# Expert 0's turn in the mixture of experts: 64 slots with fp32 products on unsplit weights, where it had 128 slots with split weights

## The chip, the cores and the metric

The kernel runs on one core of a Trainium2 chip. The time is that of the device, in microseconds, from the first to the last instruction of one execution with what lies around it; times are medians of several executions. One execution was recorded by the hardware profiler, and all rows below come from it.

## The reference

A decoder trunk of two layers over 256 tokens of width 1024, all in fp32. Each layer has a token-mixing part and then a channel mixer; the channel mixer of the second layer is a mixture of eight experts, of which each token uses its best two:

```python
logits = h @ router
top_v, top_i = lax.top_k(logits, 2)
wts = softmax(top_v)
combine = sum(one_hot(top_i, 8) * wts[..., None], axis=-2)
for e in range(8):
    y = y + combine[:, e:e+1] * ((silu(h @ w1[e]) * (h @ w3[e])) @ w2[e])
```

Here `w1[e]` and `w3[e]` are 1024 by 3584 and `w2[e]` is 3584 by 1024, so one expert has 44 MB of weights and all eight have 352 MB. Each weight is read once. With the reference's own inputs (its default seed) the reference gives the experts 0 to 7 these numbers of tokens: 60, 58, 49, 84, 77, 59, 69, 56.

## The kernel before

The mixture of experts is the function `moe`. It runs after everything else and takes the last half of the time. It works through eight **turns**, one expert each. Turn 0 is always expert 0, because its weights are fetched before the routing is known. The other seven experts are sorted by their number of tokens on the chip, and the table `RANK` gives each later turn a place in that order.

A turn gathers its expert's tokens into **slots** by a one-hot matrix `Pm`. There are two kinds of turn, told apart by `SMALL`:

- A *large* turn has 128 slots. Its weights are split by ScalarE and VectorE into a high and a low part (`hi`, `lo`, lines 1187 and 1188), and TensorE makes three fp32r products for each piece (lines 1408 to 1410 and 1426 to 1428).
- A *small* turn has 64 slots (`CAP`). It multiplies the fp32 weights as they landed (`raw`) with fp32 activations (`xs`, `as`), two halves of 64 columns of the array for each piece (lines 1404 and 1423). Nothing is split.

Before the change turns 0, 2, 4, 6 are large and 1, 3, 5, 7 small. Two neighbouring turns share one gather and one matrix `Pm` (`GROUPS`); the gather for the next pair is spread over the last step of a large turn. If an expert has more tokens than its turn has slots, all is computed again by a slow general path (`spill`); with the numbers above it isn't entered.

A turn has seven steps j, and a step three matrices (`w1`, `w3`, and `w2` of the step before), each in two **blocks** of 1 MB: 42 blocks a turn, 336 in all, numbered here from 0 in the order of their fetch. SyncE (SP) issues the transfers one after the other, in an order that the program text fixes. A block goes into one of 15 places `raw0` to `raw14`, or, once each at the start, into `acts`, `late` and `y`, which are used for other things later: 18 blocks are fetched ahead (`FIRST`), then never more than 15 are held (`MOE_BUFS`). A place comes free in a large turn when VectorE has written the block's last `lo`, in a small turn when TensorE has multiplied its last piece; `done` then fetches the next block:

```python
def fetch(most=MOE_BUFS):
    while todo and len(live) < most:
        n = slots.pop(0)
        ...
        nc.sync.dma_start(w, A["moe"][expert[e], j, b][:, h * 2048:(h + 1) * 2048])
```

For turns 1 to 7 `expert[e]` is a register. SP loads all seven from `idxi`, which VectorE computes (line 1304); this load (line 1312) stands in SP's queue between the fetches, and those behind it wait for it. Small work (the sort, the gather, the activation of a step) is laid between the pieces by a count of **ticks**, a tick for each half block multiplied. TensorE, VectorE, ScalarE and SP run in the order of the program text in this stage.

Of the kernel before, what the change touches and what calls it, by code (L numbers as in the profile page):

```python
# [9 lines left out]
F32 = mybir.dt.float32  # L10
# [4 lines left out]
ALU = mybir.AluOpType  # L15
# [3 lines left out]
P = 128  # L19
T = 256  # L20
D = 1024
KC = 8
# [5 lines left out]
NE = 8  # L28
# [29 lines left out]
NPRE = len(PRE)  # L58


RANK = [7, 0, 4, 1, 5, 2, 6, 3]
SMALL = [False, True] * 4
CAP = 64
NSMALL = sum(SMALL)
GROUPS = [(None, 0), (1, 2), (3, 4), (5, 6), (7, None)]


def constants():
    c = np.zeros((P, NCST), np.float32)

    def put(n, a):
        c[:a.shape[0], COFF[n][0]:COFF[n][0] + a.shape[1]] = a
# [10 lines left out]
    put("keyc", np.broadcast_to(np.array([1e6, 1, 2, 3, 4, 5, 6, 7])[None, :], (P, 8)))  # L83
    put("seq", np.broadcast_to(np.array(RANK)[None, :], (P, 8)))
    gmask = ((s <= t) & (i[:, None] // 64 == i[None, :] // 64)).astype(np.int32)
# [1048 lines left out]
def moe(k, l, out):  # L1134
    tc, nc, A = k.tc, k.nc, k.A
    ctx = ExitStack()
    dp = ctx.enter_context(tc.tile_pool(name="moe", bufs=1, reuse_waits="tile"))
# [31 lines left out]
    def done(block):  # L1169

        block[2] = True
        while live and live[0][2]:
            live.pop(0)
            fetch()

    def prepare(eng=nc.vector):
# [5 lines left out]
        last = q == 2048 // SUB - 1  # L1182
        if SMALL[at[0]]:
            ready.append((w[:, s], None, at + (q,), block if last else None))
# [6 lines left out]
        if last:  # L1191
            part.clear()
            blocks.pop(0)
            if not SMALL[at[0]]:
                done(block)
# [3 lines left out]
    def parts(n, kind=F32):  # L1199

        if n not in held:
            held[n] = sp.tile([P, 4, 512], kind, name=n)
        return held[n]
# [20 lines left out]
    n8, key, rank, more, idx = [S8[:, i] for i in range(5)]  # L1224
# [66 lines left out]
    def sort():  # L1291

        by = lambda a: a[:, None, :].to_broadcast([P, NE, NE])
        of = lambda a: a[:, :, None].to_broadcast([P, NE, NE])
        p, w = perm[:, 0], perm[:, 1]

        def ranks():
            nc.vector.scalar_tensor_tensor(key, n8, 8.0, k.k("keyc"), ALU.mult, ALU.add)
            nc.vector.tensor_tensor(w, of(key), by(key), ALU.is_gt)
            nc.vector.tensor_reduce(rank, w, AX.X, ALU.add)  # L1300
            nc.vector.tensor_tensor(p, by(rank), of(k.k("seq")), ALU.is_equal)
            nc.vector.tensor_tensor(w, p, by(iota[:, :NE]), ALU.mult)
            nc.vector.tensor_reduce(idx, w, AX.X, ALU.add)
            nc.vector.tensor_copy(idxi, idx)

        def turned(src, dst):
            for tt in range(2):
                nc.vector.tensor_tensor(w, p, by(src[:, tt]), ALU.mult)
                nc.vector.tensor_reduce(dst[:, tt], w, AX.X, ALU.add)

        def loads():
            _, v = nc.values_load_multi_w_load_instructions(idxi[0:1, 1:NE], engines=[mybir.EngineType.SP], min_val=0,
                                                            max_val=NE - 1)
            expert.extend(v)

        def excess():
            nc.vector.tensor_scalar(more, rank, NSMALL - 0.5, float(P - CAP), ALU.is_le, ALU.mult)
            nc.vector.tensor_tensor(n8, n8, more, ALU.add)
            nc.vector.tensor_reduce(cnt, n8, AX.X, ALU.max)
            nc.vector.tensor_copy(cnti, cnt)  # L1320

        return [ranks, loads, lambda: turned(posm, posm_s), lambda: turned(comb, comb_s), excess]
# [3 lines left out]
    def after(ticks, f):  # L1326

        tasks.append((clock[0] + ticks, f))
        tasks.sort(key=lambda t: t[0])

    def tick():
        clock[0] += 1
        while tasks and tasks[0][0] <= clock[0]:
            tasks.pop(0)[1]()

    def slots_of(g):

        Pm = dp.tile([P, 2, 2, P], F32R, name="Pm", bufs=2)
        for i, (t, io) in enumerate(zip(GROUPS[g], (iod, iota))):
            if t is not None:  # L1340
# [6 lines left out]
    def back(g, Pm, gs, PT):  # L1347
        pg = k.pg()
        here = [i for i in range(2) if GROUPS[g][i] is not None]
        for i in here:  # L1350
            for tt in range(2):
                t = GROUPS[g][i]
                c = comb_s[:, tt, t:t + 1] if t else comb[:, tt, 0:1]
# [9 lines left out]

    def places(g):

        xs = dp.tile([P, KC, CAP], F32, name="xs") if GROUPS[g][0] is not None else None
        xl = [dp.tile([P, KC, P], F32R, name=n) for n in ("xh", "xl")] if GROUPS[g][1] is not None else None
        return xs, xl

# [16 lines left out]
    def pieces(e, j, b):  # L1386
        for h in range(2):
            for q in range(2048 // SUB):
                while blocks and len(ready) <= LOOK:
                    prepare()  # L1390
                hi, lo, at, block = ready.pop(0)
                assert at == (e, j, b, h, q)
                yield (h * 2048 + q * SUB) // 512, hi, lo
                if block:
                    done(block)
                tick()

    def up(e, j, b, p, x):
        for o, hi, lo in pieces(e, j, b):
            for z in range(SUB // 512):  # L1400
                kc = o + z
                if SMALL[e]:
                    for n in range(2):
# [8 lines left out]
    def down(e, j, py, act):  # L1412
        if j == 0:
            py += [k.pc() for _ in range(1 if SMALL[e] else 2)]
        for o, hi, lo in pieces(e, j, 2):
            for n in range(2):
                for z in range(SUB // 1024):
                    c = o // 2 + z
                    s = slice(z * 1024 + n * 512, z * 1024 + n * 512 + 512)
                    first, last = j == 0 and c == 0, j == NJ - 1 and c == 3  # L1420
                    if SMALL[e]:
                        a = (c % 2) * P + (c // 2) * CAP
# [164 lines left out]
    def busy(n):  # L1587

        for _ in range(n):
            nc.tensor.matmul(idle[:, :T], ident, k.cst[:, :T], start=True, stop=True)  # L1590
# [4 lines left out]
    with tc.manual_schedule(engines=ORDERED | LOADS):  # L1595
        y = choose()
        idle = k.pj()
        busy(IDLE[0])
        pp = place()
        busy(IDLE[1])  # L1600
        for c in range(3):
            rows_of(c, y)
        rows_of(0, y, True)
        nc.vector.tensor_tensor(posm, posm, pp[:, 0:2 * NE].rearrange("p (a b) -> p a b", a=2), ALU.add)
        new = slots_of(0)
        nc.vector.tensor_copy(n8, pp[:, 2 * NE:3 * NE])
        rows_of(1, y, True)
        rows_of(2, y, True)
        to = places(0)
        for kc in range(KC):  # L1610
            gather(0, new[1], kc, to, k.pj if kc % 4 > 1 else k.pg)
        weigh()
        after(BACK, lambda: back(*new))
        for n, f in enumerate(sort()):
            after(SORT + n, f)
        group = new, to
        for e in range(NE):
            i = 0 if SMALL[e] else 1
            if e and i == 0:
                group = nxt  # L1620
            (_, _, gs, PT), (xs, x2) = group
            for j in range(NJ):
                ph = [k.pj()]
                up(e, j, 0, ph[0], x2 if i else xs)
                act, steps = hidden(e, ph)
                delay = DELAY
                if (e, j) == (NE - 1, NJ - 1):
                    delay, last = LAST, gains()
                after(delay[0], steps[0])
                ph.append(k.pj())  # L1630
                up(e, j, 1, ph[1], x2 if i else xs)
                for d, f in zip(delay[1:], steps[1:]):
                    after(d, f)
                if i == 1 and e < NE - 1:
                    g = e // 2 + 1
                    if j == NJ - 2:
                        new = slots_of(g)
                        after(BACK, lambda: back(*new))
                    if j == NJ - 1:
                        nxt = new, places(g)  # L1640
                        for kc in range(KC):
                            after(kc * 2048 // SUB // 4, lambda kc=kc, g=g, n=nxt: gather(g, n[0][1], kc, n[1]))
                if pend:
                    down(*pend[:4])
                    if pend[4]:
                        for d, f in in_turn(pend[0], *scatter(pend[0], pend[2], *pend[4])):
                            after(d, f)
                if j == 0:
                    py = []
                pend = (e, j, py, act, (gs[:, i:i + 1], PT, i) if j == NJ - 1 else None)  # L1650
        while tasks:
            tick()
        down(*pend[:4])
        banks = iter((k.pg, k.pg, k.pj, k.pj))
        finish(scatter(pend[0], pend[2], *pend[4], lambda: next(banks)()), *last)
# [64 lines left out]
    n = nc.values_load(cnti[0:1, 0:1], min_val=0, max_val=T + P)  # L1720
# [103 lines left out]
```

## Time and profile before

| | us |
|---|---|
| median of 3 runs | 1780.85 (1779.85 to 1782.62) |
| the profiled execution, its time | 1777.78 |
| the profiled execution, its span | 1776.0 |
| mixture of experts in it, first block's issue to the end | 864.8 to 1776.0 |
| its last matmuls on weights end | 1758.1 |
| TensorE busy (share of the span) | 1703.6 (96%) |
| VectorE busy | 1161.7 (65%) |
| ScalarE busy | 838.2 (47%) |

The profiled execution is 3.07 us below the median. A sum made against its rows is a sum against 1777.78, of which 1.78 lie outside the span. Busy shares are means over stages that have different limits, and a matmul's end is modelled, so TensorE's 96% doesn't say by itself that it is the bound.

### The profile page before, as it was taken

How to read it: one execution, taken by the hardware profiler on the slowest of the kernel's cores; microseconds unless marked ns; L12 is line 12 of the kernel's file. 1: busy time of each engine (PE TensorE's matmuls, PEld its weight loads, DVE VectorE, ACT ScalarE, POOL GpSimd, SP SyncE). 2: the span in 40 equal slices, each digit the busy share in tenths (PEclk: the TensorE clock that was granted, in tenths of full speed). 3: DMA queues.
4: the chain of work that ended last, by engine and by line, in shares of the span. 5: the costliest groups of instructions: out<-in, count | busy, mean ns of one | idle time of the engine just before them, and what ended most of it. 6: DMA issues, size and time to landing. Idle time of an engine off the chain costs nothing.

```text
span 1776.0 us, 30054 instructions
## 1 busy us (share of the span) xinstructions
PE 1703.6 (96%) x11915; PEld 1400.8 (79%) x11915; DVE 1161.7 (65%) x1783; ACT 838.2 (47%) x1214; POOL 50.3 (3%) x100
## 2 busy tenths in 40 slices
PE   7998989989999799999999999999999999999997
PEld 6987879989999688799977875688656876578754
DVE  3789577787876879466669950588407972289611
ACT  3653234454444743244547740477306771267501
POOL 0000010010100000000000000000000000000001
PEclk9999899999999899899989999999999999999999
DMA  9445257687874333225678989999999999999995
GB/s 347 158 165 190 73 182 259 249 287 304 314 267 145 110 129 119 73 96 190 261 307 311 366 314 421 421 421 421 418 420 421 421 421 416 421 421 421 420 421 214
DMA packets 79972, 520.92 MB, mean 293 GB/s; under 512 B 9520, under 2 KB 10160, under 8 KB 22352
## 3 DMA queue, kind: packets, MB, share of 16 engines
q1 hardware_dynamic: 67440, 476.14, 67.7%
q0 software_dynamic: 11232, 40.90, 6.7%
q8 instruction: 95, 1.56, 0.4%
q10 hardware_dynamic: 1152, 1.89, 0.3%
q14 instruction: 53, 0.43, 0.1%
HBM read 517.84 MB, written 1.05 MB: 292 GB/s over the span
## 4 chain that ended last, share of the span: by engine, by line
PE 76%; issue 8%; DMA 7%; DVE 6%; ACT 1%; POOL 0%; SPq 0%; ACTq 0%; POOLq 0%; DVEq 0%
PE pj L1404 11%; PE pj L392 7%; PE pj L393 7%; PE pj L394 7%; PE pc L1423 6%; PE pj L1408 5%; PE pj L1410 5%; PE pj L1409 5%; DMA araw<-wada 4%; PE pc L1426 3%; PE pc L1428 3%; PE pc L1427 3%; DMA raw<-moe 2%; PE pg L1453 1%; DVE lo L369 1%
## 5 line engine op out<-in xcount | busy, mean ns | idle before, releaser
L1188 DVE TENSOR_TENSOR lo<-raw,hi 128x1024 fp32r<-128x1024 f32 x330 | 396.1, 1223 | 85.0 <-ACT hi L1187 77.9
L1187 ACT ACTIVATE hi<-raw 128x1024 fp32r<-128x1024 f32 x330 | 347.5, 1059 | 128.1 <-PE pj L1409 80.0
L367 ACT ACTIVATE hi<-raw 128x1024 fp32r<-128x1024 f32 (+2 forms) x209 | 213.9, 1025 | 280.7 <-PE pj L393 207.6
L369 DVE TENSOR_TENSOR lo<-raw,hi 128x1024 fp32r<-128x1024 f32 (+2 forms) x209 | 246.5, 1181 | 77.5 <-ACT hi L367 73.9
L392 PE MATMUL pj<-hh,hi 128*128 128x256 f32 x992 | 289.9, 292 | 4.8 <-DVE t L418 3.4
L394 PE MATMUL pj<-hh,lo 128*128 128x256 f32 x992 | 285.9, 288 | 1.3 <-DVE lo L369 1.3
L393 PE MATMUL pj<-hl,hi 128*128 128x256 f32 x992 | 286.2, 289 | 0.0
L1404 PE MATMUL pj<-raw,xs 128*64 128x256 f32 x1792 | 201.4, 381 | 0.0
L392 PEld LDWEIGHTS pj<-hh,hi 128*128 128x128 f32 x992 | 191.2, 193 | 12.1 <-issue 4.8
L394 PEld LDWEIGHTS pj<-hh,lo 128*128 128x128 f32 x992 | 191.1, 193 | 2.5 <-DVE lo L369 1.8
L393 PEld LDWEIGHTS pj<-hl,hi 128*128 128x128 f32 x992 | 191.3, 193 | 2.2 <-issue 1.3
L1408 PE MATMUL pj<-hi,xh 128*128 128x512 f32 x448 | 181.3, 405 | 0.5 <-ACT hi L1187 0.5
L1410 PE MATMUL pj<-lo,xh 128*128 128x512 f32 x448 | 178.5, 398 | 2.0 <-DVE lo L1188 1.9
L1409 PE MATMUL pj<-hi,xl 128*128 128x512 f32 x448 | 177.7, 397 | 0.0
L1404 PEld LDWEIGHTS pj<-raw,xs 128*64 128x64 f32 x1792 | 125.8, 137 | 64.9 <-issue 4.7
L1448 DVE TENSOR_TENSOR late<-late,pj 128x512 f32<-128x512 f32 (+1 forms) x56 | 30.8, 550 | 207.6 <-PE pj L1404 201.0
L1410 PEld LDWEIGHTS pj<-lo,xh 128*128 128x128 f32 x448 | 84.5, 189 | 25.7 <-DVE lo L1188 5.4
L1423 PE MATMUL pc<-raw,as 128*64 128x512 f32 x448 | 102.2, 595 | 0.0
L1408 PEld LDWEIGHTS pj<-hi,xh 128*128 128x128 f32 x448 | 84.8, 189 | 21.2 <-ACT hi L1187 1.9
L1409 PEld LDWEIGHTS pj<-hi,xl 128*128 128x128 f32 x448 | 84.7, 189 | 18.7
L256 DVE SCALAR_TENSOR_TENSOR aacc<-araw,csg,aacc 128x1024 f32<-128x1024 f32 x70 | 89.6, 1280 | 8.0 <-DMA araw<-wada 7.5
L1426 PE MATMUL pc<-hi,acts 128*128 128x512 f32 x224 | 88.3, 394 | 0.0
(432 smaller groups left out, 2749.2 us busy)
## 6 DMA issues: line engine op xcount, KB each, us to landing
raw<-moe SPq DMA_DIRECT2D x333, 1024.0 KB, 18.6
raw<-win SPq DMA_DIRECT2D x43, 1024.0 KB, 5.0
araw<-wada POOLq DMA_DIRECT2D x78, 512.0 KB, 5.3
raw<-f SPq DMA_DIRECT2D x33, 1024.0 KB, 7.3
raw<-wv SPq DMA_DIRECT2D x8, 1024.0 KB, 4.8
raw<-wog SPq DMA_DIRECT2D x8, 1024.0 KB, 5.0
raw<-wad SPq DMA_DIRECT2D x6, 1024.0 KB, 7.1
raw<-wor SPq DMA_DIRECT2D x4, 1024.0 KB, 5.1
```

Of the source, the lines that this page charges most:

```text
L367: nc.scalar.activation(hi[:, :w], src, AF.Copy)
L369: nc.vector.tensor_tensor(lo[:, :w], src, hi[:, :w].bitcast(F32), ALU.subtract)
L392: nc.tensor.matmul(o, hi[:, s], ah[:, kc, :], start=kc == 0, stop=False)
L393: nc.tensor.matmul(o, hi[:, s], al[:, kc, :], start=False, stop=False)
L394: nc.tensor.matmul(o, lo[:, s], ah[:, kc, :], start=False, stop=kc == nk - 1)
L1187: nc.scalar.activation(hi, w[:, s], AF.Copy)
L1188: eng.tensor_tensor(lo, w[:, s], hi.bitcast(F32), ALU.subtract)
L1404: nc.tensor.matmul(p[64 * n:64 * n + 64, :T], x[:, kc], hi[:, z * 512 + n * T:z * 512 + n * T + T], start=kc == 0, stop=kc == KC - 1)
L1408: nc.tensor.matmul(p, x[0][:, kc], hi[:, s], start=kc == 0, stop=False)
L1409: nc.tensor.matmul(p, x[1][:, kc], hi[:, s], start=False, stop=False)
L1410: nc.tensor.matmul(p, x[0][:, kc], lo[:, s], start=False, stop=kc == KC - 1)
L1423: nc.tensor.matmul(py[0][64 * n:64 * n + 64], act[:, a:a + CAP], hi[:, s], start=first, stop=last)
```

## The change

`SMALL` makes turn 0 small too: turns 0, 1, 3, 5 and 7 have 64 slots, turns 2, 4 and 6 have 128. The group of turn 0 has the small half alone. The test for too many tokens is written anew, since the large turns are now those of rank 4, 5 and 6. The gather for turns 1 and 2 falls into the last step of turn 0 as before, but `xs` of turn 0 is still read there, so that of turn 1 is put into a free quarter of the tile `late`.

```diff
 RANK = [7, 0, 4, 1, 5, 2, 6, 3]
-SMALL = [False, True] * 4
+SMALL = [True] + [True, False] * 3 + [True]
 CAP = 64
-NSMALL = sum(SMALL)
-GROUPS = [(None, 0), (1, 2), (3, 4), (5, 6), (7, None)]
+GROUPS = [(0, None), (1, 2), (3, 4), (5, 6), (7, None)]
...
         def excess():
-            nc.vector.tensor_scalar(more, rank, NSMALL - 0.5, float(P - CAP), ALU.is_le, ALU.mult)
+            nc.vector.tensor_scalar(more, rank, -5.0, None, ALU.add)
+            nc.vector.tensor_tensor(more, more, more, ALU.mult)
+            nc.vector.tensor_scalar(more, more, 2.0, float(P - CAP), ALU.is_ge, ALU.mult)
...
     def places(g):
-        xs = dp.tile([P, KC, CAP], F32, name="xs") if GROUPS[g][0] is not None else None
+        xs = None
+        if g == 1:
+            xs = parts("late")[:, 3].rearrange("p (k n) -> p k n", k=KC)
+        elif GROUPS[g][0] is not None:
+            xs = dp.tile([P, KC, CAP], F32, name="xs")
...
-                if i == 1 and e < NE - 1:
+                if (i == 1 or e == 0) and e < NE - 1:
                     g = e // 2 + 1
```

How instructions move is shown at three places. The first is VectorE's queue where the mixture of experts begins: `R<-R,pj` makes the slot numbers, `Pm` the one-hot matrix that the gather waits for, `tl` the low part of the tokens, `lo` the low part of weights. Before:

```order
L1604 TENSOR_TENSOR R<-R,pj 128x16
L1188 TENSOR_TENSOR lo<-acts,hi 128x1024 x2
L1343 TENSOR_SCALAR Pm<-cst,R 128x128 x2
L1606 COPY S_9837<-pj 128x8
L1277 SCALAR_TENSOR_TENSOR tl<-pc,rsq,th 128x384
L1188 TENSOR_TENSOR lo<-late,hi 128x1024
L1277 SCALAR_TENSOR_TENSOR tl<-pc,rsq,th 128x384
```

The same place with the change; line 1345 is what was line 1343:

```order
L1610 TENSOR_TENSOR R<-R,pj 128x16
L1345 TENSOR_SCALAR Pm<-iod,R 128x128 x2
L1612 COPY S_9837<-pj 128x8
L1277 SCALAR_TENSOR_TENSOR tl<-pc,rsq,th 128x384 x2
L1277 SCALAR_TENSOR_TENSOR tl<-ada,rsq,th 128x256
```

The three splits `lo` are gone from between. All other splits of turn 0 are gone from this queue in the same way, so that the sort behind `idxi` follows the copy `gs` at once.

The second place is TensorE's queue at the end of the first gather (lines 1377 and 1383) and the start of turn 0. Before, three products for each piece:

```order
L1377 MATMUL pj<-Pm,tl 128x128 x2
L1408 MATMUL pj<-hi,xh 128x512
L1409 MATMUL pj<-hi,xl 128x512
L1410 MATMUL pj<-lo,xh 128x512
L1408 MATMUL pj<-hi,xh 128x512
```

With the change; line 1410 is now the small turn's product (line 1404 before), and `acts`, `late` and `raw` are blocks as they landed:

```order
L1383 MATMUL pj<-Pm,tl 128x64 x2
L1410 MATMUL pj<-acts,xs 64x256 x8
L1410 MATMUL pj<-late,xs 64x256 x8
L1410 MATMUL pj<-raw_9804,xs 64x256 x8
L1356 MATMUL pg<-R,Pm 128x1 x2
L1362 MATMUL pg<-cst,Pm 128x128 x2
L1410 MATMUL pj<-raw_9805,xs 64x256 x8
```

A block is eight such products instead of twenty-four of the other kind. Line 1356 and 1362 (the group's weights and its scatter matrix, whose copy `gs` stands ahead of the sort on VectorE) come after the third block.

The third place is SP's queue around the load of the registers; `raw6` and so on are the places, and behind "waits" stand the semaphores that the issue waits for: that of a transfer eight earlier (DMAHW) and that of the engine which frees the place. Before:

```order
L1163 DMA y_9813<-moe 128x2048 [waits DMAHW2_49]
L1163 DMA raw6_10042<-moe 128x2048 [waits DMAHW3_49,DVE_49]
L1163 DMA raw7_10074<-moe 128x2048 [waits DMAHW4_49,DVE_49]
L1312 TENSOR_LOAD idxi_9838 [waits DVE_49]
L1312 ISA x14
L1163 DMA raw8_10168<-moe 128x2048 [waits DMAHW5_49,DVE_49]
```

With the change:

```order
L1163 DMA y_9813<-moe 128x2048 [waits DMAHW2_49]
L1163 DMA raw6_10013<-moe 128x2048 [waits DMAHW3_49,PE_49]
L1312 TENSOR_LOAD idxi_9838 [waits DVE_49]
L1312 ISA x14
L1163 DMA raw7_10095<-moe 128x2048 [waits DMAHW4_49,PE_49]
L1163 DMA raw8_10114<-moe 128x2048 [waits DMAHW5_49,PE_49]
```

The load of the registers stands one fetch earlier, and the places of turn 0 are freed by TensorE instead of VectorE.

## Rows read from the trace of the kernel before

**Rows 1.** The page, its 40 slices of 44.4 us: DMA busy tenths, rate moved

```profile
DMA  9445257687874333225678989999999999999995
GB/s 347 158 165 190 73 182 259 249 287 304 314 267 145 110 129 119 73 96 190 261 307 311 366 314 421 421 421 421 418 420 421 421 421 416 421 421 421 420 421 214
```

**Rows 2.** Busy time by stretch; first row names the columns

```profile
core 0: us, PE busy (x) PEld busy (x) DVE busy (x) ACT busy (x) POOL busy (x), PEclk, DMA share, GB/s
...
929.00:1121.00 192.00, 188.14 (x1085) 133.41 (x1085) 112.70 (x138) 96.58 (x123) 0.00 (x0) 1.00 0.91 357
1121.00:1331.00 210.00, 208.63 (x1186) 146.86 (x1184) 122.37 (x136) 105.83 (x132) 0.00 (x0) 1.00 1.01 420
```

**Rows 3.** Waits of SP's queue, 929 to 1121: total us, times, longest

```profile
SPq L1163 <- DVE lo L1188: 83.7, 32, 5.5
...
SPq L1312 <- DVE lo L1188: 7.9, 1, 7.9
```

**Rows 4.** All waits of TensorE's matmuls, 1121 to 1752

```profile
PE pg L1360 <- DVE gs L1355: 2.5, 3, 1.1
PE pg L1377 <- DVE xl L1384: 1.2, 2, 0.6
```

**Rows 5.** Last block fetched ahead: its issue (timeline), issue to landing (page)

```profile
909.31 0.33 SPq L1163 DMA_DIRECT2D y<-moe  x1
...
y<-moe SPq DMA_DIRECT2D x1, 1024.0 KB, 19.9
```

**Rows 6.** Line 1163 at 1100.5, first block of turn 2: issue, landing

```profile
L1163 SPq DMA_DIRECT2D raw<-moe x1: 333/333/333, 1100.5 to 1100.5; - x1
...
DMA to landing us min/median/max: 20.4/20.4/20.4
```

**Rows 7.** Line 1163 at 1734.2, the last block: issue, landing

```profile
L1163 SPq DMA_DIRECT2D raw<-moe x1: 333/333/333, 1734.2 to 1734.2; - x1
...
DMA to landing us min/median/max: 20.6/20.6/20.6
```

**Rows 8.** Line 1163 at 927.3, block 19: issue, landing

```profile
L1163 SPq DMA_DIRECT2D raw<-moe x1: 328/328/328, 927.3 to 927.3; - x1
...
DMA to landing us min/median/max: 6.8/6.8/6.8
```

**Rows 9.** Line 1312, load of the registers on SP's queue: first and last start

```profile
L1312 SPq SEQ_ASSERT  x7: 18/18/28, 936.4 to 938.0; - x7
L1312 SPq TENSOR_LOAD <-idxi x1: 1663/1663/1663, 934.5 to 934.5; - x1
```

**Rows 10.** Chain that ended last, one step of turn 1: start, us

```profile
1082.12 7.06 PE pj L1404 x64
1089.18 3.43 PE pc L1423 x16
...
1092.98 7.06 PE pj L1404 x64
```

**Rows 11.** Timeline: first steps of the stage, and the sort's result

```profile
906.66 2.35 DVE L1188 TENSOR_TENSOR lo<-acts,hi 128x1024 fp32r<-128x1024 f32 x2
...
916.23 0.73 PE L1408 MATMUL pj<-hi,xh 128*128 128x512 f32 x1
...
934.27 0.17 DVE L1304 CAST idxi<-S 128x8 int32<-128x8 f32 x1
```

**Rows 12.** Timeline of TensorE: start of turn 2, end of the last products

```profile
1125.32 0.48 PE L1408 MATMUL pj<-hi,xh 128*128 128x512 f32 x1
...
1752.71 5.37 PE L1423 MATMUL pc<-raw,as 128*64 128x512 f32 x24
```

**Rows 13.** Busy time by stretch where the clock was high and low

```profile
134.00:172.00 38.00, 31.85 (x216) 28.56 (x215) 36.01 (x64) 14.65 (x25) 2.65 (x5) 1.00 0.60 211
190.00:206.00 16.00, 16.00 (x144) 14.80 (x144) 5.46 (x10) 3.11 (x6) 0.00 (x0) 0.50 0.20 67
910.00:920.00 10.00, 9.95 (x38) 8.99 (x38) 5.99 (x21) 4.20 (x10) 0.00 (x0) 0.50 1.01 422
```

## Prediction

> **What bounds the kernel now.** I read the page's 40 slices first, because a mixture of experts streams its weights once and the question is whether the transfers or TensorE set the pace. In the reader's eye should stay one edge: from the 25th slice on the rate stands at 420 GB/s, slice after slice, to the last but one; the three slices before it moved 311, 366 and 314 [rows 1]. The mixture begins in slice 21, so its first two turns run below the rate that the rest holds.
>
> The same cut by turns: from 929 to 1121, that is from the last block fetched ahead to the first block of turn 2, the core moved 357 GB/s on average; from 1121 on, 420 [rows 1, 2]. The blocks themselves confirm the ends: block 17 was issued at 909.3 and landed 19.9 later, at 929.2 [rows 5]; block 82, the first of turn 2, was issued at 1100.5 and landed at 1120.9 [rows 6].
>
> Next I asked who holds the transfers back before 1121. SP's queue waited 83.7 us in 32 waits for `lo`, the split that frees a place, and 7.9 us more at the load of the registers [rows 3]. So turn 0 is bound by TensorE with the split in its train: places come free at the pace of a large turn, and the transfers wait for places.
>
> Behind 1121 both limits are reached at once: the transfers run at 420 GB/s, and TensorE's matmuls wait 3.7 us in 631 [rows 2, 4], in two groups of waits. That matters for the sum: from turn 2 on nothing changes in the order or the kind of work, so the whole tail from there can at best move forward as one piece, by the smaller of two amounts: how much earlier block 82 lands, and how much earlier TensorE can start turn 2.
>
> **The change, step by step.** *The transfers.* Between the landings of block 17 and block 82 lie 191.7 us [rows 5, 6] and 65 blocks of 1.049 MB. At 420 GB/s a block takes 2.50 us and 65 take 162.3: 29.4 us less. The stretch's own mean gives nearly the same: 192 us at 357 GB/s are 68.5 MB, 163.2 us at 420, 28.8 less [rows 2]. I take 29. It asks that no issue comes too late any more.
>
> *Are the places free in time?* A small turn's step of six blocks takes 10.86 us, 1.81 a block (7.06 us for four blocks of `w1` and `w3`, 3.43 for two of `w2`) [rows 10], below the 2.50 of a transfer. So once turn 0 runs as a small one, TensorE frees places faster than blocks land, and 15 places are never full. Nothing else in the stretch holds SP but the start.
>
> *The start.* VectorE no longer makes the two `lo` (2.35 us) ahead of `Pm` [rows 11], so the first gather starts some 2 us earlier; its products are half as wide and the low parts `xl` are gone. Turn 0's first product stood at 916.2 [rows 11]. Bounds for it now: 914 (only the 2.35 gained) and 911 (of the 7.2 us from the end of these `lo` to that product, which are mostly the gather, 3 gained as well). I take 912, nearer to the second, since every part of the gather shrinks. TensorE's clock is low there, granted 0.50 from 910 to 920 [rows 13], that is 1.2 GHz; a block then costs up to 3.5 us instead of 1.77. To 920 two and a bit blocks are done, the third by about 921.5, the fourth by 923. The fetch of block 18 waits for the third, the register load for `idxi`, which VectorE makes after the copy behind the third block: the copy and the sort's seven small operations, which I put at 0.25 us each from the cast that ends them [rows 11], make 923.6. The load with its register steps took from 934.5 to 938.0 [rows 9], 3.6 us, so block 19 is issued at 927.2. That happens to be when it was issued before, and then it landed 6.8 us later, at 934.1 [rows 8], just behind block 18. So the hole that the load makes now, behind block 19, closes: `idxi` came at 934.3 [rows 11], more than ten later than I expect it. If the first products are at 914, block 19 is some 2 us late; I book 1 us.
>
> *TensorE up to turn 2.* From 912: two small turns at seven steps of 10.86 are 152 us; the eight wide gathers, the products of `back` and the scatter of turn 0, some 50 products, are 9 at the mean of 0.18 us (208.6 for 1186) [rows 2], and I put them at 8 to 13; the low clock to 920 adds 4. Sum 1076 to 1081. Block 82 lands at 1121 minus 29, at 1092. So TensorE waits for transfers in most of turn 1, and is there in time with 11 us to spare.
>
> *The seam at turn 2.* Its first product stood at 1125.3 [rows 12], 4.4 us behind the landing of its block, because TensorE still had turn 1's blocks to do. Now TensorE waits, and the seam is landing plus one `hi` (1.1) and part of one `lo` (1 us): 1094, 31 earlier. The transfers' 29 is the smaller one.
>
> *The end.* The last block was issued at 1734.2 and landed at 1754.8 [rows 7]; TensorE ended its products at 1758.1 [rows 12], 3.3 behind, of which a last block needs 1.7. So this slack of 1.6 us lets the end move by up to 30.5 where the landings move by 29. I take 29.5.
>
> *Costs at nothing.* Two small operations more in `excess` (0.2 us each) run on a VectorE that loses 84 splits of 1.2 us in turn 0. The gate, product and turn of turn 0 become those of a small turn, which turn 1 already has. `xs` in `late` adds no wait that the products show in their order. ScalarE loses as many splits and gains nothing. Eighteen blocks fetched ahead, and what gates them, stay as they were.
>
> Sum: 29.5 less 1 for the start is 28.5; 1777.78 minus 28.5 is 1749.3 in an execution like the profiled one, which lay 3.07 below the median. **Predicted: 1752.**
>
> **A page against the rows.** The rate of 420 GB/s is what the sum rests on; rows show it from the 25th slice to the last but one [rows 1]. The Trainium skill, "DMA: Bandwidth & Descriptors", section "Where 436 GB/s comes from", says that loads from HBM are bound by the HBM's share of a core, about 358 GB/s. By that figure, as an estimate, 65 blocks take 190 us and the change saves 1 to 2 us, the outcome of rival two. The trace disagrees, with 420 against 358, and the sum goes by the trace.
>
> **Rivals.** *One, slower: the clock stays low.* In turn 1 TensorE now works 1.8 us and waits 0.7 us a block. The clock has fallen elsewhere: it stood at 0.50 from 190 to 206 with TensorE busy throughout [rows 13]. Against it: from 134 to 172 TensorE was busy only 31.9 of 38 us at 1.00, and at 0.50 a block takes 3.5 us, more than a transfer, so TensorE would be busy without a break, as it was from 910 to 920 before its clock rose [rows 13]. TensorE needs about 162 us for turns 0 and 1 and has 180 until 1092: 36 us of low clock are free. After that each costs half. At 98 us nothing is gained, and if both turns ran low (2 times 162 from 912) turn 2 would start at 1236, 111 later: 1892. From 106 us of low clock on it is slower by over 0.2%. The Trainium skill, "TensorE: Matmul & The Clock Gate", section "HAM oscillation — how this bites in real kernels", describes such a case: where short bursts of matmuls alternate with waits for DMA, the clock falls in every gap and each burst starts cold. By it turn 1 could run low throughout; no run here has shown a small turn that waits. Chance 4 in 100.
>
> *Two, no change: the stream before 1121 is held by the memory and not by places.* Then the 357 GB/s [rows 2] stay, turn 0 ends early, TensorE waits more, and block 82 lands at 1120: 1780. Against it stand the 83.7 us of waits for `lo` [rows 3] and 420 right behind. 2 in 100.
>
> *Three, part of it: the hole at the register load stays.* Block 20 could be issued only behind the load, at 938.0, when block 19 had been at 927.3 [rows 8, 9], where one block every 2.5 us would do. If `idxi` is late again, or the clock stays low into the first steps so that places come slowly, 3 to 8 us are left: 1755 to 1760. 12 in 100.
>
> *Four: the clock falls at the seam.* TensorE is the bound from turn 2 on, and 10 us low there, as from 910 to 920 [rows 13], cost 5: 1757. 8 in 100. *Five: expert 0 has more than 64 tokens*, and the general path streams everything again. The reference gives 60; well under 1 in 100, if that.
>
> **The numbers.** Forecast (27 to 31 us less, 1750 to 1754): 74 in 100. A measurement of this kernel tells about 0.2%, 3.6 us, from no change. Faster: the forecast, three and four, 0.94; same: 0.02; slower: 0.04. Downward there is little: 421 GB/s in place of 420 and the tail's whole 1.6 are 31.4 less, 1749.5, and runs scatter by 1 to 2 us about their median. Upward the range takes in three and four, also where they meet, and leaves one and two out: 1746 to 1763.
>
> **What would show it.** Right: 929 to about 1092 at 418 to 421 GB/s; SP waiting for TensorE or for earlier landings, not for a split; the first product of turn 0 at 911 to 914; TensorE idle 11 to 18 us up to turn 2, most of it in turn 1 and ended by DMA; the first product of turn 2 at 1093 to 1095; from there the same 631 us. Wrong: a stretch of clock 0.50 in turns 0 to 2; a gap in the landings at blocks 18 to 20; a rate below 410 in the stretch with SP not waiting for places; a shift at turn 2 of 29 that is given back later, at the seams of turns 4 and 6.

## The result, and the profile after

| | us |
|---|---|
| before, median of 4 runs (lowest to highest) | 1780.96 (1779.85 to 1782.62) |
| after, median of 4 runs | 1752.76 (1751.44 to 1755.93) |
| ratio, after to before (95% interval) | 0.9843 (0.9826 to 0.9861) |
| the profiled execution after, its time and span | 1755.93, 1754.2 |

All medians and ratios in this document leave out one slow execution, of the run without low products below: 1813.51 us, at a granted clock of 0.818.

The forecast was 1752, 28.5 less in the profiled execution; the medians differ by 28.2. The two profiled executions differ by only 21.9 (1777.78 and 1755.93). The first question is therefore where in the trace that time lies.

The page of after, in the 40 slices of [rows 1], now of 43.9 us (PEclk is the share of TensorE's full clock that was granted, in tenths):

```profile
PEclk9999898999999799899999999999999999999999
DMA  9445247678784333215479999999999999999995
GB/s 341 170 147 202 85 146 263 232 269 331 297 297 169 103 137 103 97 50 185 172 288 421 421 421 421 420 421 421 421 420 421 421 419 420 421 421 422 419 421 225
```

The edge has moved to the front: the rate stands at 419 to 422 from the 22nd slice to the last but one. The 22nd begins at 921, 1 us behind the first product of turn 0, so turns 0 and 1 have no slow slice any more.

Line 1163 of after, issue and landing of blocks 17, 19, 82 and 335, as in [rows 5 to 8]:

```profile
L1163 SPq DMA_DIRECT2D y<-moe x1: 328/328/328, 918.2 to 918.2; - x1
DMA to landing us min/median/max: 19.8/19.8/19.8
...
L1163 SPq DMA_DIRECT2D raw<-moe x1: 332/332/332, 932.9 to 932.9; - x1
DMA to landing us min/median/max: 10.1/10.1/10.1
...
L1163 SPq DMA_DIRECT2D raw<-moe x1: 332/332/332, 1081.4 to 1081.4; - x1
DMA to landing us min/median/max: 19.7/19.7/19.7
...
L1163 SPq DMA_DIRECT2D raw<-moe x1: 333/333/333, 1714.6 to 1714.6; - x1
DMA to landing us min/median/max: 19.7/19.7/19.7
```

Block 17 lands at 938.1 (before: 929.2), block 82 at 1101.1 (1120.9), block 335 at 1734.3 (1754.8). From 17 to 82 that is 163.0 us where it was 191.7; from 82 to 335 it is 633.2 where it was 633.9. Block 19 lands at 943.0, two transfers behind block 17, so the hole behind the register load is gone.

Busy time by stretch, between block 17 and block 82 and in the first 210 us behind it, with the columns of [rows 2]:

```profile
938.00:1101.00 163.00, 147.67 (x1058) 77.32 (x1054) 11.94 (x33) 14.51 (x42) 0.00 (x0) 1.00 1.01 421
1101.00:1311.00 210.00, 206.88 (x1172) 146.22 (x1174) 122.48 (x136) 105.48 (x132) 0.00 (x0) 1.00 1.01 421
```

The waits of SP's queue from 938 to 1101, then those of TensorE's matmuls from 919 to 1102:

```profile
SPq L1163 <- DMA raw<-moe: 121.2, 62, 3.3
SPq L1163 <- PE pj L1410: 4.2, 5, 1.8
```

```profile
PE pj L1410 <- DMA raw<-moe: 9.3, 18, 2.0
PE pc L1429 <- DMA raw<-moe: 5.4, 10, 0.6
```

SP's 83.7 us of waits for a split [rows 3] have become waits for earlier landings, which only say that the transfers run back to back. TensorE waits for a landing 28 times: once for each of blocks 54 to 81, the last 28 ahead of turn 2, which are multiplied as they land. Before, it had a store of landed blocks there.

The timeline of after: first product of turn 0, `idxi`, first product of turn 2, last products, as in [rows 11, 12]; below it the load of the registers, as in [rows 9]:

```profile
919.88 1.38 PE L1410 MATMUL pj<-acts,xs 128*64 128x256 f32 x8
...
929.10 0.17 DVE L1304 CAST idxi<-S 128x8 int32<-128x8 f32 x1
...
1102.23 0.50 PE L1414 MATMUL pj<-hi,xh 128*128 128x512 f32 x1 [1.27 <-ACT hi L1187]
...
1731.03 5.37 PE L1429 MATMUL pc<-raw,as 128*64 128x512 f32 x24
```

```profile
L1312 SPq SEQ_ASSERT  x7: 18/18/28, 931.2 to 932.8; - x7
L1312 SPq TENSOR_LOAD <-idxi x1: 1663/1663/1663, 929.3 to 929.3; - x1
```

Measured from the landing of block 17, the last products end 798.3 us behind it (1736.4 less 938.1); before it was 828.9 (1758.1 less 929.2). The stage is 30.6 us shorter. But block 17 landed 8.9 us later in this execution than in the one before, in stages that the change doesn't touch, and 30.6 less 8.9 is, to 0.1, the 21.8 by which the spans differ. Whether those 8.9 belong to the change had to be tried.

### The profile page after: what moved, and what is told of

Its sections match the earlier page's. It is cut to its first block, busy times and chain, and to the rows that moved or that the text cites. A ratio compares the mean times of both kernels' runs of the same rounds, so it can differ in the third digit from the quotient of the medians.

```text
span 1754.2 us, 29823 instructions
## 1 busy us (share of the span) xinstructions
PE 1668.6 (95%) x11957; PEld 1348.0 (77%) x11957; DVE 1054.3 (60%) x1684; ACT 747.7 (43%) x1129; POOL 50.3 (3%) x100
## 4 chain that ended last, share of the span: by engine, by line
PE 80%; DVE 9%; DMA 8%; ACT 1%; issue 1%; SPq 0%; DVEq 0%; ACTq 0%
PE pj L1410 11%; PE pj L392 8%; PE pj L393 8%; PE pj L394 8%; DMA raw<-moe 6%; PE pc L1429 6%; PE pj L1414 4%; PE pj L1416 4%; PE pj L1415 4%; PE pc L1432 2%; PE pc L1434 2%; PE pc L1433 2%; DVE lo L369 2%; PE pg L1459 1%; DMA araw<-wada 1%
## 5 line engine op out<-in xcount | busy, mean ns | idle before, releaser
L1188 DVE TENSOR_TENSOR lo<-raw,hi 128x1024 fp32r<-128x1024 f32 x252 | 302.3, 1222 | 71.0 <-ACT hi L1187 65.6
L1187 ACT ACTIVATE hi<-raw 128x1024 fp32r<-128x1024 f32 x252 | 265.1, 1059 | 112.4 <-PE pj L1415 52.4
L1454 DVE TENSOR_TENSOR late<-late,pj 128x256 f32<-128x256 f32 (+1 forms) x56 | 29.0, 517 | 281.0 <-PE pj L1410 274.5
L1414 PE MATMUL pj<-hi,xh 128*128 128x512 f32 x336 | 135.4, 403 | 1.3 <-ACT hi L1187 1.3
L1429 PE MATMUL pc<-raw,as 128*64 128x512 f32 x560 | 129.1, 596 | 5.4 <-DMA raw<-moe 5.4
L1416 PE MATMUL pj<-lo,xh 128*128 128x512 f32 x336 | 133.1, 396 | 0.6 <-DVE lo L1188 0.5
L1415 PE MATMUL pj<-hi,xl 128*128 128x512 f32 x336 | 132.7, 395 | 0.0
L1429 PEld LDWEIGHTS pc<-raw,as 128*64 128x64 f32 x560 | 38.7, 137 | 71.0 <-issue 58.4
L392 PE MATMUL pj<-BK,hi 128*128 128x256 f32 (+1 forms) x280 | 80.8, 294 | 0.9 <-ACT BK L993 0.9
L393 PE MATMUL pj<-vt,hi 128*128 128x256 f32 (+1 forms) x280 | 80.3, 291 | 0.0
```

The source lines that it names most:

```text
L392: nc.tensor.matmul(o, hi[:, s], ah[:, kc, :], start=kc == 0, stop=False)
L393: nc.tensor.matmul(o, hi[:, s], al[:, kc, :], start=False, stop=False)
L1187: nc.scalar.activation(hi, w[:, s], AF.Copy)
L1188: eng.tensor_tensor(lo, w[:, s], hi.bitcast(F32), ALU.subtract)
L1414: nc.tensor.matmul(p, x[0][:, kc], hi[:, s], start=kc == 0, stop=False)
L1415: nc.tensor.matmul(p, x[1][:, kc], hi[:, s], start=False, stop=False)
```

## Experiments

The runs were made in three sets. In each the kernel before ran on the same chip, with medians of 1779.24, 1779.46 and 1779.27.

**The changed kernel again, in two sets: do the 8.9 us ahead of the stage belong to it?** No edit.

> The changed kernel unaltered, beside the others and for a second profile. Theory (from turn 0 on the transfers set the pace, 2.50 us a block from the first block fetched to the last): 1752.8 again, and the mixture takes the same time from the issue of its eighth block to its last product, 829 us, wherever that issue falls. Rival (the stages ahead of the mixture got slower by the change, 9 us in its first profile): the eighth block is issued at 907 again, against 898 before.

> The changed kernel as it is, to be compared with the two above on one chip. All theories: 0.981 to 0.986 of the kernel before.

Measured: 1748.84, ratio 0.9825 (0.979 to 0.9859), and 1750.02, 0.9832 (0.9815 to 0.9849). Block 17 was issued at 911.1 and 911.6 and landed at 931.0 and 931.4, so the 8.9 of the first profile are 1.8 and 2.2 here: scatter from one execution to the next. The eighth block was issued at 900.1 and 900.5, not at 907, and the last product ended 829.1 and 829.7 behind it, as the theory had it. The stage behind it took the same as in the first profile: the last products ended 798.3 and 798.7 us behind block 17. By the medians the change is worth 28.2 us in the first comparison, 30.4 and 29.3 in these two.

**Turns 2, 4 and 6 without the products of the low part of the weights: what sets the pace behind turn 1?**

```diff
                 nc.tensor.matmul(p, x[0][:, kc], hi[:, s], start=kc == 0, stop=False)
-                nc.tensor.matmul(p, x[1][:, kc], hi[:, s], start=False, stop=False)
-                nc.tensor.matmul(p, x[0][:, kc], lo[:, s], start=False, stop=kc == KC - 1)
+                nc.tensor.matmul(p, x[1][:, kc], hi[:, s], start=False, stop=kc == KC - 1)
```

> The changed kernel, in which turns 2, 4 and 6 leave out the product with the low part of the weights, a third of their products: 168 a turn at 0.222 us, 37 us a turn, 112 in all. The output is less exact. Theory: transfers set the pace, so 0 to 3 us less (the seam at turn 2 and the tail), 1750 to 1753. Rival (from turn 2 on TensorE still sets the pace, as its busy time of 99% says): 112 less, 1641; something between if the two share it.

Measured: 1751.37, 0.9833 (0.9791 to 0.9876), no gain beside the 1748.84 of the changed kernel. Busy time from turn 2 to the end, the changed kernel (first of the two runs above), then this one:

```profile
1094.00:1729.00 635.00, 629.48 (x3556) 441.07 (x3556) 364.79 (x398) 315.14 (x389) 2.90 (x8) 1.00 1.01 417
```

```profile
1095.00:1732.00 637.00, 558.11 (x3060) 346.62 (x3056) 355.36 (x398) 305.99 (x390) 2.90 (x8) 0.98 1.00 417
```

TensorE is busy 71 us less and the stretch is as long: behind turn 1 of the changed kernel the transfers set the end. So TensorE's 629 of 635 is no bound. What the change gains must come from landings that come earlier, as the prediction had it.

**Useless products in turn 1, few and many, in both kernels: how much slack has TensorE?** At the start of each step of turn 1, 3 products that nobody reads (12 in the third run); the trace holds two records for each. The edit with 3 was made to the kernel before as well.

```diff
+                if e == 1:
+                    w = k.ps.tile([P, 512], F32, name="ada")
+                    for _ in range(3):
+                        nc.tensor.matmul(w[:, :T], ident, k.cst[:, :T], start=True, stop=True)
```

> The changed kernel with three products of no use (fp32, 256 columns, about 0.48 us each) ahead of each of the seven steps of turn 1: 10 us of work. Theory: TensorE waits 15 us for transfers there, so 0 to 2 us more, 1753 to 1755. Rival (TensorE sets the pace): 10 more, 1763.

> The kernel before, with 10 us of products that nobody reads added to turn 1 on TensorE, as in the run on the changed kernel where they cost nothing. Theory (before, TensorE is behind the transfers from turn 0 on and works off the blocks that wait): the end moves by 8 to 11 us. Rival (turn 1 has slack before as well, and only the splits held turn 0): 0 to 2 us.

> The same with twelve such products a step, 84 in all, about 40 us. Theory: 40 less the 15 that TensorE waits and less some 2 of slack at the seam, so 23 more, 1776. Rival (TensorE sets the pace): 40 more, 1793.

The groups of these products by line, in the changed kernel with 3 products a step, in the one before with 3, and in the changed one with 12 (count, then busy us and mean ns):

```profile
L1632 PE MATMUL ada<-cst 128*128 128x256 f32 x42 | 10.2, 380 | 0.0
```

```profile
L1626 PE MATMUL ada<-cst 128*128 128x256 f32 x42 | 10.2, 380 | 0.0
```

```profile
L1632 PE MATMUL ada<-cst 128*128 128x256 f32 x168 | 37.4, 379 | 0.0
```

The same 10.2 us cost nothing after the change (1749.40 beside 1748.84, ratio 0.983, 0.979 to 0.987) and 9.0 before it (1788.31 beside 1779.27, ratio 1.0051, 1.0034 to 1.0068). That pair of runs shows most plainly what the change did: before, TensorE's work in turn 1 stood on the path to the end; after, some 10 us more of it don't reach that path.

With 37.4 us the time was 1763.97, 0.9904 (0.9868 to 0.994): 15.1 more by the medians, and 12.8 more in the trace, from the landing of block 17 to the last products. The theory had expected 23 more, the rival 40, so the slack was mis-sized. The first product of turn 2, the changed kernel and this one:

```profile
1095.07 0.50 PE L1414 MATMUL pj<-hi,xh 128*128 128x512 f32 x1 [1.27 <-ACT hi L1187]
```

```profile
1111.04 0.48 PE L1414 MATMUL pj<-hi,xh 128*128 128x512 f32 x1
```

From the issue of the eighth block (900.1 and 901.5) that is 195.0 and 209.5, 14.5 later, so 37.4 less 14.5, some 23 us, were hidden. The waits shown for TensorE are 14.7 in 28 landings, and the busy column leaves 15.3 of 163 idle. Both are too low; the likely reason, not tested, is that a matmul's end is modelled, so that part of a wait is shown as work. A third reading fits better: 28 blocks land 2.50 apart where TensorE needs 1.81 [rows 10], 19.3 us, and at the seam it waits for the first splits of turn 2, 1.3 and more.

**One of three products in turn 0 of the kernel before, and the unread splits kept in the changed one: what did the products cost, what the splits?**

```diff
-                nc.tensor.matmul(p, x[0][:, kc], hi[:, s], start=kc == 0, stop=False)
+                nc.tensor.matmul(p, x[0][:, kc], hi[:, s], start=kc == 0, stop=e == 0 and kc == KC - 1)
+                if e == 0:
+                    continue
...
+        if at[0] == 0:
+            hi, lo = [sp.tile([P, SUB], F32R, name=n, bufs=SPLIT_MOE) for n in ("hi", "lo")]
+            nc.scalar.activation(hi, w[:, s], AF.Copy)
+            eng.tensor_tensor(lo, w[:, s], hi.bitcast(F32), ALU.subtract)
```

The first piece is the edit to the kernel before (`w2` the same way), the second, alone, that to the changed kernel.

> The kernel before, in which turn 0 leaves out two of the three products of each piece (those with the low part of the tokens and of the weights); the splits stay. The output is less exact. TensorE then needs 0.9 us a block in turn 0, and VectorE with 2.55 frees the places. Theory (TensorE set the pace of turn 0): VectorE takes over just below it, 42 blocks by 0.2 to 0.3 us are 8 to 12 less, 1767 to 1771 beside 1779. Rival (VectorE's split set it): no change, 1779.

> The changed kernel, in which ScalarE and VectorE still make all 84 splits of turn 0 that no product reads, in their old places in the program. A place is then freed by TensorE's last product as in the change, but in the order that VectorE's work allows: 2.45 us a block and some 0.1 for the rest, 2.55, against 1.81 of TensorE and 2.50 of a transfer. Theory (turn 0 must free places no slower than blocks land; the kernel before lost the time because three products a piece took 2.7 to 2.8 us a block): 3 to 10 more than the changed kernel, 1752 to 1759 beside its 1749. Rival (VectorE's split, not TensorE, held the places before): nearly all of the gain is lost, 1775 to 1780.

Measured: the kernel before with one product took 1765.95, 0.9925 (0.9904 to 0.9946), 13.5 less, a little over what was expected. The changed kernel with the splits took 1758.37, 0.9879 (0.985 to 0.9907), 9.5 over the 1748.84 of the changed kernel by the medians, and 7.0 in the traces, from the landing of block 17 to the last products. Both runs make the splits and give TensorE less to do; none has the three products without the splits, so what the splits alone cost beside the products isn't shown. From block 17 to block 82 it is 175.0 us with one product and 170.0 with the unread splits, between the 191.7 of before and the 163.0 of the change. In the changed kernel with splits, two stretches of turn 0, the group of the splits on VectorE, and the longest waits of SP's queue and of TensorE:

```profile
932.00:943.00 11.00, 5.70 (x30) 3.24 (x32) 10.42 (x29) 6.67 (x9) 0.00 (x0) 0.69 0.56 214
943.00:990.00 47.00, 38.60 (x270) 19.63 (x266) 47.00 (x44) 43.84 (x47) 0.00 (x0) 0.96 1.01 422
```

```profile
L1186 DVE TENSOR_TENSOR lo<-raw,hi 128x1024 fp32r<-128x1024 f32 x78 | 89.9, 1214 | 10.0 <-ACT hi L1185 10.0
```

```profile
SPq L1163 <- DVE lo L1186: 59.1, 34, 2.5
...
SPq L1316 <- DVE lo L1186: 8.6, 1, 8.6
...
PE pg L1463 <- DVE late L1458: 16.6, 6, 5.3
```

VectorE is busy 47.00 of 47.00: two splits a block are 2.43 us, which together with the small work fills the 2.5 of a transfer. The `idxi` of the sort and the step's activation (`late`, line 1458) queue behind splits. That opens the hole at the register load again (214 GB/s from 932 to 943) and makes TensorE wait up to 5.3 us. The hole is most of the loss: block 19 lands 7.0 us behind block 18 instead of 2.5, 4.5 of the 7.0 us, while from 943 to 990, with VectorE full, the rate is 422. So a full VectorE by itself didn't slow the transfers there. The expectation that TensorE's last product would free each place didn't hold either: SP waited 59.1 us for `lo`, which reads the block too, and 30.5 for products of line 1414.

The kernel before, from 929 to 1020, and the same with one product, from 932 to 1020:

```profile
929.00:1020.00 91.00, 88.44 (x390) 69.92 (x388) 83.09 (x96) 70.39 (x74) 0.00 (x0) 1.00 0.90 340
```

```profile
932.00:1020.00 88.00, 60.53 (x166) 34.53 (x166) 84.77 (x102) 70.91 (x77) 0.00 (x0) 0.75 0.98 396
```

With a third of the products VectorE becomes the fullest engine (84.77 of 88) and the rate rises from 340 to 396 only. TensorE waits there for splits and for `late` (up to 3.7 us), at a granted clock of 0.75. The old turn 0 had two engines nearly full, TensorE at 97% and VectorE at 91% of the stretch, and neither run that keeps the splits holds 421 over the whole of turns 0 and 1.

**The sort at tick 0 in the kernel before: was the hole at the register load worth anything there?**

```diff
-SORT = 8
+SORT = 0
```

> The kernel before with the sort laid at the first tick of turn 0 instead of the eighth, so that the register load doesn't hold up SP; the hole of 7.5 us between blocks 19 and 20 should close. Theory (before, TensorE has 33 to 43 us of landed blocks ahead of it in turn 0, and the lost transfers come from the places): 0 to 2 less, 1777 to 1779. Rival (the hole at the register load is a part of its own of the 29): 7 less, 1772.

Measured: 1779.34, 0.9993 (0.9976 to 1.001), no change. The load now starts at 925.5 and is done 2 us before the next fetch at 931.1 gets its place, but the largest wait of SP's queue from 934 to 1123 is

```profile
SPq L1163 <- DVE lo L1188: 93.1, 35, 5.5
```

against 83.7 and 7.9 in [rows 3], together 91.6: the wait at the load has become a wait for a split. A hole in the transfers costs nothing while places set their pace.

**Another order of the places fetched ahead, then the sort at tick 0 with it: can the changed kernel go on earlier still?** The first order leaves `y` to the last and lets block 7 wait for a place that comes free late. The new one takes those first that come free first.

```diff
-FIRST = ["acts", "late"] + [f"raw{i}" for i in (6, 7, 8, 4, 5, 12, 13, 14, 9, 10, 11, 2, 3, 1, 0)] + ["y"]
+FIRST = ["acts", "late"] + [f"raw{i}" for i in (6, 7, 8, 4, 5)] + ["y"] + [f"raw{i}" for i in (9, 10, 11, 2, 3, 1, 0, 13, 14, 12)]
```

> The changed kernel with another order of the places that are filled ahead: the place that waits for the last statistics of the mixer (raw12, 24 us of waiting on SP, with raw13 and raw14 behind it) goes to the end and y, raw9, raw10 come first. Theory (the transfers set the pace from the first block on, so each us by which the stream starts earlier is a us less): if these three are free when the queue reaches them, the two or three blocks fit into the 8 us before the old issue in which the transfers lie idle, 3 to 7 less, 1742 to 1746 beside 1749; the eighth block's issue in the trace says by how much, and the end moves by the same. Rival (an earlier start only makes TensorE's lead smaller): same as the changed kernel although the blocks land earlier. If the places aren't free earlier, nothing moves and nothing is told apart.

> The changed kernel with the new order of the places fetched ahead, unchanged from the earlier run, beside which it was 2.7 us faster by the medians of two calls and 5.7 us faster in the stage's traces. Theory (the seven blocks that can be issued earlier land earlier, and all landings move by that): 3 to 6 us below the changed kernel in the same call. Rival (the difference was scatter ahead of the stage): within 1.5 us.

> The changed kernel with the places fetched ahead in the new order (that of the run before it), and the sort laid at tick 0 behind the gather instead of tick 8, so that SP loads the registers while it waits for a place anyway. In the new order the landings showed a gap of some 6 us at blocks 18 to 20: block 18 was issued when turn 0's first place came free, and behind it the register load took 3.6 us. Theory (the transfers set the end, so every us of the gap is a us of the time): half the gap goes, 2 to 3.5 us less than the new order alone. Rival (the gap is made by the full places alone, and TensorE's first products set it): no difference, within 1 us, or 1 to 2 us more, since the sort now stands ahead of other small work on VectorE.

The new order took 1746.13, 0.9816 (0.979 to 0.9842), and in the later set 1743.65, 0.9811 (0.979 to 0.9833), beside 1750.02, 0.9832 (0.9815 to 0.9849), of the changed kernel there. The largest group of waits of SP's queue ahead of turn 0, then first block and `y`, in the changed kernel and in the new order (both of the later set):

```profile
SPq L1163 <- PE ada L321: 24.3, 1, 24.3
```

```profile
867.03 0.42 SPq L1163 DMA_DIRECT2D acts<-moe  x1
...
911.56 0.33 SPq L1163 DMA_DIRECT2D y<-moe  x1
```

```profile
SPq L1163 <- DVE lo L369: 18.8, 3, 7.0
```

```profile
866.57 0.43 SPq L1163 DMA_DIRECT2D acts<-moe  x1
...
878.88 0.33 SPq L1163 DMA_DIRECT2D y<-moe  x1
```

The wait of 24.3 for `ada` is 5.8 in the new order, and `y`, which was block 17, is block 7. Block 17 lands 13.1 us earlier, measured from the first issue, but the last products end only 5.9 earlier. All 18 places are now full before TensorE has multiplied the third block: block 18 is issued at 918.2, 17 us behind block 17. With the load of the registers behind it, blocks 18 and 19 land 5.3 and 5.9 us behind the block ahead of each instead of 2.5.

The sort at tick 0 beside it gave 1743.04, 0.9792 (0.9775 to 0.9809): 0.6 less than the new order by the medians, where 2 to 3.5 were expected. Its profile can't settle why: the load was done at 921.6 and block 18 issued at 922.1, as the theory asks, but the granted clock was 0.50 from 916 to 918 where the run of the order alone had 1.00, and turn 0's first block took 3.18 us instead of 1.95. From the first issue to the last products it was 857 us in both. Whether the sort is worth 2 us stays open; that order and sort together beat the changed kernel is shown (0.9809 against 0.9815 at the nearest ends of the intervals). For the order alone the intervals overlap.

## Why the prediction was right, point by point

**The transfers, 29: right.** 191.7 less 163.0 is 28.7, at 421 GB/s. Rival two (the memory holds the stream) fell with it. The rate that the sum took from [rows 1] was the right one, where the Trainium skill, "DMA: Bandwidth & Descriptors", section "Where 436 GB/s comes from", has some 358 GB/s for loads from HBM (it also names 425 as measured for one transfer of 16 MB). The trace disagrees with the 358: the stage held 421 up to block 82 and, in the changed kernel run again, 417 over the 635 us behind it.

**The start, 1 us lost: better than booked.** The first product came 18.2 us ahead of the landing of block 17, against 13.0 before: 911.0 on the clock of the first profile, the lower bound of 911 to 914. `idxi`, at 929.1, is 920.2 on that clock (forecast 923.6), and block 19's issue 924.0 (forecast 927.2). The low clock of this turn ended at 915.0 on that clock, where the forecast had let it run to 920; in the two later profiles of the changed kernel it lasted as short or wasn't there. No landing was late at blocks 18 to 20, so rival three didn't happen and the 1 us wasn't lost. (One later block, 66, landed 1.3 us late.) That the load could have made a hole was right: it did in the run with the splits, and in the new order, where places were full.

**TensorE up to turn 2, 11 to 18 us idle: the place right, the size too low.** It waited in turn 1, at each of the last 28 landings. The idle time that the trace shows, 14.7 to 15.3, is within the forecast, but the slack is some 23 us (37.4 useless us moved turn 2 by 14.5). The step that was too large is the sum of TensorE's work from 912 to 1076 or 1081, 164 to 169 us, with 4 for the low clock and 8 to 13 for the gathers. From 919.9 to 1102.2 less the 23 it was some 159; the clock was low for 3.4 us only, which costs half of that, so the gathers were under 6. Nothing hung on it, since the transfers were the smaller gain.

**The seam, 1094: right.** 1102.23 less 8.9 is 1093.3, with block 82 landed 1.1 us before. The seam moved by 32.0 us and the landing of block 82 by 28.7; the end moved by the stage's 30.6, so the smaller of the two, with the slack of the tail, did set it.

**The end: right.** Behind block 82 the landings gained another 0.7 (633.9 to 633.2), and the last products end 2.1 behind the last landing where it was 3.3, 1.2 of the 1.6 that the tail had. 28.7, 0.7 and 1.2 are the 30.6 of the stage. The forecast booked 28.5: 29, 0.5 for the tail, less 1 for the start.

**The clock, rivals one and four: it stayed high, though rival four came close.** In the profiled execution it was granted 0.50 only from 920.5 to 923.9 in turns 0 to 2; from 1020 to 1100, with TensorE waiting at every block from 1030 on, 1.00 throughout. Of the two reasons given, the stretch from 134 to 172, with pauses at 1.00 [rows 13], points the way the runs went; that a slow TensorE would be a busy one and so recover wasn't needed, since the clock never fell behind the waits for landings. At the seam TensorE waits 1.27 and then 0.52 us for the first splits. In the three profiles of the changed kernel the clock stayed at 1.00 there. In the run with 10.2 us of useless products it fell behind waits of the same length; the first product of turn 2 and the stretch behind it:

```profile
1094.88 0.50 PE L1414 MATMUL pj<-hi,xh 128*128 128x512 f32 x1 [1.27 <-ACT hi L1187]
```

```profile
1097.00:1101.00 4.00, 4.00 (x12) 3.13 (x11) 2.96 (x4) 2.59 (x4) 0.00 (x0) 0.57 1.00 418
```

It was 0.50 for 3.4 us, and the last products ended 799.2 us behind block 17 instead of 798.3, so little was lost. But the same waits came out both ways, and that the clock held at this seam was in part luck. It also fell where TensorE waited longer for VectorE: 0.75 on average over 88 us in the kernel with one product, 0.69 from 932 to 943 in the one with unread splits, and six times behind turn 1 in the run without low products, around waits of 1.1 to 2.4 us. So the mechanism is real. The three profiles of this change show no fall of the clock from turn 1 to the last products.

**What the gain is made of.** In the traces, from the landing of block 17 on, leaving out two of three products, with the splits kept, saved 18.1 of the 30.6, and the splits, put back into the changed kernel, cost 7.0. By the medians these are 13.5 and 9.5 of some 30, so each is known to a few us only. The 5.5 between (some 7 by the medians) belong to neither by itself; that they are the waits of TensorE for splits and its lower clock in the run with one product was argued from the waits, not tried apart. The prediction's reading, that turn 0 was bound by TensorE with the split in its train, holds for more than half of the gain by the traces and a little under half by the medians. That VectorE stood close behind it left out, at no cost, since the change lifts both.

## What to carry to other kernels

Look for the stretch in which the stream runs below the rate that it holds elsewhere, and ask who frees its places; the gain is the missing bytes at the full rate, and it lasts to the end only if whatever follows is bound by the same stream. Before giving a turn to one engine's budget, add up the next fullest engine too: cutting TensorE's products alone left 12.5 of the 30.6 us, with VectorE busy 84.77 of 88. A few microseconds of useless work in the disputed stretch, in both kernels, tell a bound from slack far better than a busy share does.

## What the runs showed of the hardware that was not expected

The clock didn't fall in a stretch where TensorE waited at each of 28 blocks in a row for a DMA: 0.69 us each by the sum above, granted clock 1.00. With waits up to 5.3 us on VectorE in turn 0 it fell, to 0.69 in the stretch around them. In between the runs give no rule: behind two waits of 1.27 and 0.52 it fell in one run and not in the others. The Trainium skill, "TensorE: Matmul & The Clock Gate", section "HAM oscillation — how this bites in real kernels", describes a clock that falls in the gaps of a matmul loop that waits for DMA. There each wait is longer than the burst of work before it; in turn 1 it is shorter, 0.69 after 1.81, which the prediction, in rival one, passed over. So the 28 short waits don't contradict that section, and no run here shows a loop like the one it describes.

The busy column hid a good quarter of the idle time: 16.6 us by the column up to the first product of turn 2 (15.3 to 1101 and the wait at the seam), some 23 by the useless products that fitted in.

Stages that the change doesn't touch took some 7 us more or less from one execution of the same kernel to the next (block 17 of the changed kernel landed at 938.1, 931.0 and 931.4), so two profiles whose times differ by 22 us held a change of 30.6.
